# The experts of a two-layer backbone as one list of weight tiles, with fixed places for small operations and a fourth split buffer

## The chip, the cores and the metric

The kernel runs on one NeuronCore of a Trainium2 chip. The metric is the device time of one execution in microseconds. Five engines work beside one another: PE (TensorE) multiplies, VectorE (DVE) and ScalarE (ACT) do elementwise work, GpSimd (POOL) is almost unused here, and SyncE (SP) issues the transfers. Each engine runs its instructions in the order of its own list and waits in that list.

## The reference, cut to what matters

Two layers of a hybrid backbone for 256 latent and 256 context tokens of width 1024. The change is in the last block of the second layer, a top-2-of-8 mixture of SwiGLU experts over the 256 latent tokens:

```python
logits = (xs @ router_w) + router_b
top_val, top_idx = lax.top_k(logits, 2)
gates = sum(one_hot(top_idx, 8) * softmax(top_val)[..., None], axis=-2)
for e in range(8):                       # w_gate, w_up 1024 x 2816, w_down 2816 x 1024, float32
    y = y + gates[..., e:e + 1] * ((silu(xs @ w_gate[e]) * (xs @ w_up[e])) @ w_down[e])
```

The 24 weight matrices are 277 MB of float32, read once each.

## The kernel before, in words

**Precision.** A float32 product is made from float32r products of two parts: `hi` is the value rounded to float32r and `lo` the rest. `hilo` (line 634) makes them from a loaded tile `raw`: ScalarE copies to `hi` (L635), then VectorE subtracts to `lo` (L636). For each weight tile of 128 x 2048 (1 MB) there is one transfer, one `hi` and one `lo`. The buffers are rings: six for `raw`, three for `hi` and three for `lo` in the expert stage (`open_ring(st, 6, 3, 2048)`). A `hi` buffer is free when the products that read it have ended, a `raw` buffer when its `lo` is made.

**Experts.** `route` (line 1421) counts the tokens of each expert and sorts the experts by count. The first four in that order are *big* ones (places for 128 tokens), the other four *small* (64 tokens). A big expert's tokens are the stationary operands `xghi` and `xglo`, so each slice of a tile takes three matmuls: `xghi` by `hi`, `xghi` by `lo`, `xglo` by `hi`. A small expert has both parts of its 64 tokens side by side in one operand `xs`, and takes two matmuls a slice; the halves are added afterwards by a matmul with `sum2`. They run in turn: big 0, small 4, big 1, small 5 and so on.

`gather` (line 1543) makes a one-hot matrix from the places and multiplies it with the tokens, for a big and a small expert at once. `expert_up` (line 1586) goes through six chunks of columns; a chunk of 512 columns has two gate tiles and two up tiles. After a big chunk: `h` = silu(gate) on ScalarE, times up on VectorE (L1632, L1633), four transposes on PE (L1635), and a split into `hT` (L1639, L1640). After a small one: copies `h` and `u` of both sums (L1615, L1616), the sums on PE (L1619), silu and product `g` (L1622, L1623), and a split into `hS` (L1628, L1629). `expert_down` (line 1645) takes eleven tiles. Its tiles are interleaved with the next expert's up tiles, one after every two: `experts` (line 1503) drives both as generators. `scatter` (line 1672) adds the result to the residual with another 16 matmuls.

**What sets the order.** The program only gives a priority, its order of tracing. A planner places each instruction on its engine's list by a cost model, dependencies and free buffers, and can so move a small operation ahead of or behind others. `prefetch` (line 1255) loads the first three tiles into buffers of another pool, ahead of the router; with the six `raw` buffers nine tiles are loaded early.

Of the kernel before, what the change touches and what calls it, by code (L numbers as in the profile page):

```python
# [9 lines left out]
F32 = mybir.dt.float32  # L10
# [10 lines left out]
KD = 8  # L21
# [141 lines left out]
class Kernel:  # L163
# [175 lines left out]
    def ssq_add(self, pool, tag, bank, m, segs, bufs=3, direct=False):  # L339
        nc = self.nc  # L340
        n = segs[-1][1]
        sq = pool.tile([P, T], F32, tag=tag, name="nsq", bufs=bufs)[:, :n]
# [844 lines left out]
    def odd_out(self, od):  # L1187
# [6 lines left out]
        self.sorted = self.mp.tile([P, 6, NE], F32, name="sorted")  # L1194
        self.ints = self.mp.tile([P, 1 + 2 * NE], I32, name="ints")
        self.y2 = [flat[1][:, i * D:i * D + D] for i in range(2)]
        with ExitStack() as st:
# [28 lines left out]
            def back(m, ps):  # L1226
                r = self.resl[:, m]
                nc.vector.scalar_tensor_tensor(r, ps, mix[2][:, m, 0:1], r, op0=ALU.mult, op1=ALU.add)
                xm = yp.tile([P, L], F32, tag="xg", name="xg", bufs=3)
                nc.scalar.activation(xm, r, AF.Copy, scale=gs[:, m, 0:1])  # L1230
                self.ssq_add(yp, "sq", ssq, m, [(0, L, r)])
# [22 lines left out]

    def prefetch(self):
        self.ahead = {}
        for i in range(3):
            src = ("m_gate", "m_up")[i // 2]
            self.ahead[src, i % 2] = self.load(self.I[src][i % 2], self.mp, "big", 3)
# [161 lines left out]
    def route(self, xp, lg, cm, tag):  # L1421
# [35 lines left out]
        pg = tile_(6, NE)  # L1457
# [3 lines left out]
        nc.vector.tensor_scalar(pos, pos, -1.0, None, op0=ALU.add)  # L1461
        nc.vector.tensor_copy(pg[:, 4], cm["order"])
# [14 lines left out]
        nc.vector.tensor_tensor(pg[:, 2:4], rr, den[:, :, None].to_broadcast([P, 2, NE]), op=ALU.mult)  # L1477
# [4 lines left out]
        self.pos, self.gate = self.sorted[:, 0:2], self.sorted[:, 2:4]  # L1482
# [3 lines left out]
        ints = xp.tile([P, 1 + 2 * NE], I32, name="ints")  # L1486
# [7 lines left out]
        nc.vector.tensor_copy(self.ints, ints)  # L1494
# [7 lines left out]

    def experts(self, wk):
        got = {0: self.gather(wk, self.pos, 0, NB)}
        order = [p + NB * s for p in range(NB) for s in range(2)]
        down, todo = iter(()), None
        for n, p in enumerate(order):
            small, i = divmod(p, NB)
            x, hT = got[i][small], []
            for c, _ in enumerate(self.expert_up(wk, p, x, hT)):  # L1510
                if c == 0 and todo:
                    self.scatter(wk, *todo)
                    todo = None
                if c == 2 and small and i + 1 < NB:
                    got[i + 1] = self.gather(wk, self.pos, i + 1, NB + i + 1)
                for done in down:
                    todo = done
                    break
            for done in down:
                todo = done  # L1520
            down = self.expert_down(wk, p, x, hT)
        self.scatter(wk, *todo)
        for todo in down:
            pass
        self.scatter(wk, *todo, "gu")
        self.finish(wk)

    def overflow(self, wk):
        with self.tc.If(self.most > 0):
            for p in range(NE):  # L1530
                over = self.nc.values_load(self.ints[0:1, 1 + NE + p:2 + NE + p], min_val=0, max_val=L)
                with self.tc.If(over > 0):
                    pos = wk.tile([P, 2, NE], F32, tag="pos2", name="pos2", bufs=1)
                    self.nc.vector.tensor_scalar(pos, self.pos, float(-P if p < NB else -64), None, op0=ALU.add)
                    x, hT = self.gather(wk, pos, p, None)[0], []
                    for _ in self.expert_up(wk, p, x, hT, False):
                        pass
                    for todo in self.expert_down(wk, p, x, hT, False):
                        pass
                    self.scatter(wk, *todo)  # L1540
            self.finish(wk)

    def gather(self, wk, pos, p, s):
        nc = self.nc
        mm = nc.tensor.matmul
        cm = self.cm
        hot = wk.tile([P, 2, 2, P], F32R, tag="hot", name="hot", bufs=2)
        both = [(1, p, "slot")] + ([] if s is None else [(0, s, "slot2")])
        for b in range(2):
            for i, e, slot in both:  # L1550
                nc.vector.tensor_scalar(hot[:, b, i], cm[slot], pos[:, b, e:e + 1], None, op0=ALU.is_equal)
        xg = [wk.tile([P, KD, P], F32R, tag="xg" + n, name="xg" + n, bufs=1) for n in ("hi", "lo")]
        xs = None if s is None else wk.tile([P, KD, P], F32R, tag="xs", name="xs", bufs=2)
        cols = slice(0, 2) if xs is not None else slice(1, 2)
        for j, (src, dst) in enumerate(zip((self.thi, self.tlo), xg)):
            for k in range(0, KD, 2):
                ps = self.bank("tr").rearrange("p (k i w) -> p k i w", k=2, i=2)
                for kk in range(2):
                    c = slice((k + kk) * P, (k + kk + 1) * P)
                    for b in range(2):  # L1560
                        mm(ps[:, kk, cols], lhsT=src[:, b, c], rhs=hot[:, b, cols], start=b == 0, stop=b == 1)
                parts = [(dst[:, k:k + 2], ps[:, :, 1])]
                if xs is not None:
                    parts.append((xs[:, k:k + 2, 64 * j:64 * j + 64], ps[:, :, 0, 0:64]))
                for o, i in parts:
                    if j:
                        nc.vector.tensor_copy(o, i)
                    else:
                        nc.scalar.activation(o, i, AF.Copy)
        ps = self.bank("tr").rearrange("p (i b w) -> p i b w", i=2, b=2)  # L1570
        hotT = wk.tile([P, 2, L], F32R, tag="hotT", name="hotT", bufs=2)
        for i, _, _ in both:
            for b in range(2):
                nc.tensor.transpose(ps[:, i, b], hot[:, b, i].bitcast(F32), self.ident)
        nc.scalar.activation(hotT[:, cols], ps[:, cols].rearrange("p i b w -> p i (b w)"), AF.Copy)
        ps = self.bank("tr")
        for i, e, _ in both:
            for b in range(2):
                mm(ps[:, i:i + 1], lhsT=hot[:, b, i].bitcast(F32), rhs=self.gate[:, b, e:e + 1], start=b == 0,
                   stop=b == 1)  # L1580
        gs = wk.tile([P, 2], F32, tag="gslot", name="gslot", bufs=2)
        nc.vector.tensor_copy(gs[:, cols], ps[:, cols])
        big = (xg, hotT[:, 1], gs[:, 1:2])
        return [big] if xs is None else [big, ((xs,), hotT[:, 0], gs[:, 0:1])]

    def expert_up(self, wk, p, now, hT, ahead=True):
        nc = self.nc
        mm = nc.tensor.matmul
        xg = now[0]
        small = len(xg) == 1  # L1590
        for c in range(6):
            width, ks = (512, 4) if c < 5 else (256, 8)
            pgu = []
            for name in ("m_gate", "m_up"):
                ps = self.bank("gu")
                for t in range(8 // ks):
                    j = 2 * c + t
                    raw = self.ahead.pop((name, j), None) if ahead and p == 0 else None
                    whi, wlo = self.weights(None if raw is not None else self.wsrc(name, p, j), ks, raw)
                    for k in range(ks):  # L1600
                        kk = t * ks + k
                        o = ps[:, :width]
                        mm(o, lhsT=xg[0][:, kk], rhs=whi(k), start=kk == 0, stop=False)  # L1603
                        mm(o, lhsT=xg[0][:, kk], rhs=wlo(k), start=False, stop=small and kk == 7)  # L1604
                        if not small:
                            mm(o, lhsT=xg[1][:, kk], rhs=whi(k), start=False, stop=kk == 7)  # L1606
                pgu.append(ps)
                if c < 5:
                    yield
            n = width // P  # L1610
            h = wk.tile([P, 512], F32, tag="h", name="h", bufs=2)
# [117 lines left out]
```

## Time and profile before

| | us |
|---|---|
| median of 3 runs | 1937.38 |
| their range | 1935.64 to 1937.73 |
| the profiled execution | 1935.74 |
| its span, first to last instruction | 1933.9 |

All times in rows are microseconds from the start of the span, and durations in microseconds unless they are marked ns. A row of a timeline has start, duration, engine, line, operation, the tiles it writes and reads, the number of instructions merged into it, and in brackets the idle time ahead of it with what ended it. The end of a matmul is modelled, so the start of the next one tells more than its duration. PEld is the weight load of PE, which runs ahead of the matmuls.

### The profile page before, as it was taken

What the parts mean: (1) busy time and instruction counts of PE and PEld (TensorE: products, weight loads), DVE (VectorE), ACT (ScalarE), POOL (GpSimd) and SP (SyncE); (2) the same over time, 40 slices, a digit from 0 to 9 for tenths busy, and PEclk for the clock granted to TensorE, in tenths of its full rate; (3) what the DMA queues carried; (4) which work ended last, traced back from release to release, by engine and by line L of the source; (5) the groups of instructions that cost most, each with busy time, mean ns of one, the idle gap of its engine ahead of it and who ended that gap; (6) DMA issues with size and microseconds to landing.
All of it is one profiled execution on the core that took longest, in us unless ns stands there. A gap on an engine that the chain in (4) does not pass through costs nothing.

```text
span 1933.9 us, 28843 instructions
## 1 busy us (share of the span) xinstructions
PE 1768.6 (91%) x11628; PEld 1390.4 (72%) x11628; DVE 1445.9 (75%) x1966; ACT 1006.3 (52%) x1131; POOL 90.3 (5%) x92
## 2 busy tenths in 40 slices
PE   6989999698999999989999879989999899998996
PEld 3657776377888888778876768777777677777775
DVE  4577888657995383456685678888888889888987
ACT  3433325635232222366562357776677677767774
POOL 0011102200000000002110000000000000000000
PEclk8999999798999999989999889999999999999997
DMA  7232111325666163123203339999999999989993
GB/s 291 91 111 88 46 42 49 109 88 200 236 238 239 66 223 125 66 80 109 87 23 146 144 133 359 363 344 363 345 341 363 353 346 341 370 335 360 352 380 119
DMA packets 57310, 409.32 MB, mean 212 GB/s; under 512 B 6480, under 2 KB 6864, under 8 KB 8016
## 3 DMA queue, kind: packets, MB, share of 16 engines
q1 hardware_dynamic: 57168, 407.39, 56.5%
q8 instruction: 93, 1.52, 0.3%
q14 instruction: 49, 0.40, 0.1%
HBM read 406.32 MB, written 1.05 MB: 211 GB/s over the span
## 4 chain that ended last, share of the span: by engine, by line
PE 71%; DVE 17%; ACT 7%; issue 4%; POOL 1%; DMA 0%; SPq 0%; DVEq 0%; ACTq 0%; POOLq 0%
DVE lo L636 10%; PE bank_gu L1604 6%; PE bank_b L234 6%; PE bank_b L235 6%; PE bank_b L236 6%; PE bank_gu L1603 5%; ACT hi L635 5%; PE bank_mm L234 4%; PE bank_mm L235 4%; PE bank_mm L236 4%; PE bank_gu L1606 3%; PE bank_dn L1660 3%; PE bank_dn L1659 2%; PE bank_dn L1662 1%; PE bank_tr L1619 1%
## 5 line engine op out<-in xcount | busy, mean ns | idle before, releaser
L636 DVE TENSOR_TENSOR lo<-raw,hi 128x2048 fp32r<-128x2048 f32 (+1 forms) x398 | 765.4, 1946 | 186.3 <-ACT hi L635 184.2
L635 ACT ACTIVATE hi<-raw 128x2048 fp32r<-128x2048 f32 (+1 forms) x398 | 641.3, 1632 | 276.0 <-PE bank_b L235 140.5
L1604 PE MATMUL bank_gu<-lo,xghi 128*128 128x512 f32 (+1 forms) x384 | 148.9, 388 | 27.2 <-DVE lo L636 26.7
L1604 PE MATMUL bank_gu<-lo,xs 128*128 128x512 f32 (+1 forms) x384 | 146.2, 387 | 7.5 <-DVE lo L636 6.4
L1603 PE MATMUL bank_gu<-hi,xghi 128*128 128x512 f32 (+1 forms) x384 | 145.6, 379 | 0.0
L1606 PE MATMUL bank_gu<-hi,xglo 128*128 128x512 f32 (+1 forms) x384 | 144.5, 376 | 0.0
L1603 PE MATMUL bank_gu<-hi,xs 128*128 128x512 f32 (+1 forms) x384 | 144.3, 382 | 0.2
L234 PE MATMUL bank_b<-xhi,hi 128*128 128x512 f32 x352 | 138.0, 394 | 2.9 <-ACT xhi L635 2.9
L234 PE MATMUL bank_mm<-xhi,hi 128*128 128x512 f32 (+1 forms) x320 | 120.9, 380 | 21.5 <-ACT hi L635 15.3
L235 PE MATMUL bank_b<-xlo,hi 128*128 128x512 f32 x352 | 137.9, 392 | 0.0
L236 PE MATMUL bank_b<-xhi,lo 128*128 128x512 f32 x352 | 137.6, 391 | 0.0
L236 PE MATMUL bank_mm<-xhi,lo 128*128 128x512 f32 (+1 forms) x320 | 118.3, 370 | 2.9 <-DVE lo L636 2.1
L235 PE MATMUL bank_mm<-xlo,hi 128*128 128x512 f32 (+1 forms) x320 | 119.7, 374 | 0.0
L1604 PEld LDWEIGHTS bank_gu<-lo,xghi 128*128 128x128 f32 x384 | 72.2, 188 | 54.0 <-DVE lo L636 41.6
L1604 PEld LDWEIGHTS bank_gu<-lo,xs 128*128 128x128 f32 x384 | 72.4, 188 | 32.6 <-DVE lo L636 21.2
L312 DVE SCALAR_TENSOR_TENSOR ada<-ada_raw,sT,ada 128x1024 f32<-128x1024 f32 x70 | 87.2, 1282 | 5.5 <-DMA ada_raw<-in_ada_v 4.8
L234 PEld LDWEIGHTS bank_mm<-xhi,hi 128*128 128x128 f32 x320 | 62.4, 196 | 37.2 <-ACT hi L635 16.5
L1603 PEld LDWEIGHTS bank_gu<-hi,xghi 128*128 128x128 f32 x384 | 72.3, 188 | 13.5
L1603 PEld LDWEIGHTS bank_gu<-hi,xs 128*128 128x128 f32 x384 | 72.4, 188 | 12.4 <-ACT hi L635 1.5
L1606 PEld LDWEIGHTS bank_gu<-hi,xglo 128*128 128x128 f32 x384 | 72.4, 188 | 12.2
L234 PEld LDWEIGHTS bank_b<-xhi,hi 128*128 128x128 f32 x352 | 66.5, 189 | 17.0 <-ACT xhi L635 3.2
L1660 PE MATMUL bank_dn<-lo,hT 128*128 128x512 f32 x176 | 72.8, 414 | 6.2 <-DVE lo L636 6.2
(512 smaller groups left out, 3461.0 us busy)
## 6 DMA issues: line engine op xcount, KB each, us to landing
raw<-in_m_up SPq DMA_DIRECT2D x88, 1024.0 KB, 7.2
raw<-in_m_gate SPq DMA_DIRECT2D x88, 1024.0 KB, 7.1
raw<-in_m_down SPq DMA_DIRECT2D x88, 1024.0 KB, 7.3
ada_raw<-in_ada_v SPq DMA_DIRECT2D x28, 1024.0 KB, 4.9
raw<-in_ada SPq DMA_DIRECT2D x20, 1024.0 KB, 6.0
raw<-in_o_in SPq DMA_DIRECT2D x16, 1024.0 KB, 4.9
raw<-in_w_in SPq DMA_DIRECT2D x12, 1024.0 KB, 4.9
raw<-in_f_gate SPq DMA_DIRECT2D x11, 1024.0 KB, 5.8
```

The costliest lines, as they stand in the source:

```text
L234: mm(out, lhsT=whi, rhs=xhi, start=start, stop=False)
L235: mm(out, lhsT=whi, rhs=xlo, start=False, stop=False)
L236: mm(out, lhsT=wlo, rhs=xhi, start=False, stop=stop)
L312: nc.vector.scalar_tensor_tensor(acc[r], w[:, k], s, acc[r], op0=ALU.mult, op1=ALU.add)
L635: self.nc.scalar.activation(hi, x, AF.Copy)
L636: (self.nc.gpsimd if pool else self.nc.vector).tensor_tensor(lo, x, hi.bitcast(F32), op=ALU.subtract)
L1603: mm(o, lhsT=xg[0][:, kk], rhs=whi(k), start=kk == 0, stop=False)
L1604: mm(o, lhsT=xg[0][:, kk], rhs=wlo(k), start=False, stop=small and kk == 7)
L1606: mm(o, lhsT=xg[1][:, kk], rhs=whi(k), start=False, stop=kk == 7)
L1619: mm(ps[:, 256 * i + 64 * j:256 * i + 64 * j + 64], lhsT=t[:, j * P:(j + 1) * P], rhs=self.cm["sum2"], start=True, stop=True)
L1659: mm(py[a], lhsT=h[0], rhs=whi(i)[:, half[a]], start=f == 0, stop=False)
L1660: mm(py[a], lhsT=h[0], rhs=wlo(i)[:, half[a]], start=False, stop=len(h) == 1 and f == FT - 1)
```

## The change

The tiles of all experts become one list, `tiles()`, in the same order as before (two up tiles, one down tile of the expert before). `pipeline` walks it. At step n it emits what is due ahead of the split, then the split of tile n+3, the transfer of tile n+9, the products of tile n, what is due behind them, and one step of a queue of gather and scatter pieces. `pin` is `keep_in_program_order`: the instruction may not be placed ahead of the one traced before it on its engine. It stands at the splits, the products and the small operations of the stage; the transfers are not pinned. The split rings get a fourth buffer each. The gather of expert 0 is made alone, from the unsorted places (expert 0 is always first), and its one-hot operations are traced ahead of the sort; the first small expert's gather is a second one, of which one step runs per tile. Some work buffers change: `xs` lies in freed space of `flat[0]`, `u` and `hot` have one buffer, `hotT` and `gslot` three, `g` uses `h`, and the squares buffer of the router's norm is 256 wide. The path for more tokens than places (`overflow`) is rewritten likewise; its branch does not run in the trace.

```diff
-    def hilo(self, hi, lo, x, pool=False):
-        self.nc.scalar.activation(hi, x, AF.Copy)
-        (self.nc.gpsimd if pool else self.nc.vector).tensor_tensor(lo, x, hi.bitcast(F32), op=ALU.subtract)
+    def hilo(self, hi, lo, x, pool=False, pin=lambda ins: ins):
+        pin(self.nc.scalar.activation(hi, x, AF.Copy))
+        pin((self.nc.gpsimd if pool else self.nc.vector).tensor_tensor(lo, x, hi.bitcast(F32), op=ALU.subtract))
...
+        nc.vector.tensor_tensor(pg[:, 2:4], rr, den[:, :, None].to_broadcast([P, 2, NE]), op=ALU.mult)
+        self.hots = {}
+        self.hot(0, pg, 0, None)
         nc.vector.tensor_copy(pg[:, 4], cm["order"])
...
+    LEAD = 3
+
+    def prefetch(self):
+        jobs = self.tiles()
+        self.raws = {m: self.fetch(jobs[m], self.mp, "big", 3) for m in range(3)}
+        for m in range(3, 9):
+            self.raws[m] = self.fetch(jobs[m])
+        self.halves = {m: self.split(self.raws.pop(m), lambda ins: ins) for m in range(self.LEAD)}
+
     def experts(self, wk):
...
+        self.got = {p: {} for p in range(NE)}
+        for f in self.gather(wk, 0, self.plain, 0, None):
+            f()
+        self.pipeline(wk, self.tiles(), True)
         self.finish(wk)
+
+    def pipeline(self, wk, jobs, main=False):
...
+        lead, ring = self.LEAD, 9 if main else 6
...
+        if main:
+            self.hot(1, self.sorted, None, NB)
+            queue += self.gather(wk, 1, self.sorted, None, NB)
+        n = 0
+        while n < len(jobs) or queue or any(m >= n for m in list(pre) + list(post)):
+            for f in pre.pop(n, ()):
+                f()
+            if n + lead < len(jobs):
+                halves[n + lead] = self.split(raws.pop(n + lead), pin)
+            if n + ring < len(jobs):
+                raws[n + ring] = self.fetch(jobs[n + ring])
+            if n < len(jobs):
+                name, p, c, t, k = jobs[n]
+                for where, slot, f in self.product(wk, jobs[n], halves.pop(n), n):
+                    {"pre": pre, "post": post, "queue": queue}[where].setdefault(slot, []).append(f) \
+                        if where != "queue" else queue.extend(f)
+                if main and name == "m_gate" and p >= NB and p < NE - 1 and c == 1 and t == 0:
+                    i = p - NB + 1
+                    self.hot(i, self.sorted, i, NB + i)
+                    queue += self.gather(wk, i, self.sorted, i, NB + i)
+            for f in post.pop(n, ()):
+                f()
+            if queue:
+                more = queue.pop(0)()
+                if more:
+                    pre.setdefault(n + 1, []).append(more)
+            n += 1
...
+        def part(j, k):
+            src = (self.thi, self.tlo)[j]
+            ps = self.bank("tr").rearrange("p (k i w) -> p k i w", k=2, i=2)
+            for kk in range(2):
+                c = slice((k + kk) * P, (k + kk + 1) * P)
+                for b in range(2):
+                    pin(mm(ps[:, kk], lhsT=src[:, b, c], rhs=hot[:, b], start=b == 0, stop=b == 1))
...
+            def turn():
+                got["ps"] = ps = self.bank("tr")
+                for i, a in enumerate((h, u)):
+                    for j in range(m):
+                        pin(mm(ps[:, 256 * i + 64 * j:256 * i + 64 * j + 64], lhsT=a[:, j * P:(j + 1) * P],
+                               rhs=self.cm["sum2"], start=True, stop=True))
...
+            return [("pre", n + 1, first), ("post", n + 1, turn), ("pre", n + 2, second), ("pre", n + 3, third)]
...
+        return [("pre", n + 1, first), ("post", n + 1, turn), ("pre", n + 2, second)]
...
+        steps = [lambda: None] + [lambda m=m: back(m) for m in range(0, KD, 2)]
+        return [("pre", n + 1, take), ("queue", 0, steps)]
...
-            self.open_ring(st, 6, 3, 2048)
+            self.open_ring(st, 6, 4, 2048)
```

For a small expert `first` is the two copies `h` and `u`, `second` the silu and product `g`, `third` the split into `hS`. For a big one `first` is `h`, `turn` the four transposes and `second` the split into `hT`. The two `return` lines are those of a small and of a big chunk, the last one is that of the last down tile. A gather has ten steps (eight parts, the transposes of the one-hot, the gates), a scatter four.

## Rows read from the trace of the kernel before

**Rows 1.** The page's first part: busy us of each engine, share of the span, instructions.

```profile
PE 1768.6 (91%) x11628; PEld 1390.4 (72%) x11628; DVE 1445.9 (75%) x1966; ACT 1006.3 (52%) x1131; POOL 90.3 (5%) x92
```

**Rows 2.** Stretches: length, busy PE, PEld, DVE, ACT, POOL; clock, DMA share, GB/s.

```profile
1129.08:1196.59 67.51, 67.51 (x338) 56.05 (x337) 55.18 (x44) 48.00 (x37) 0.00 (x0) 1.00 0.78 287
1196.59:1290.97 94.38, 90.65 (x461) 72.70 (x459) 83.92 (x65) 69.95 (x61) 0.00 (x0) 1.00 0.95 368
...
1389.89:1489.07 99.18, 93.61 (x474) 74.50 (x472) 88.42 (x71) 72.10 (x63) 0.00 (x0) 1.00 0.94 352
1489.07:1588.04 98.97, 89.91 (x416) 70.94 (x414) 84.97 (x56) 68.01 (x48) 0.00 (x0) 1.00 0.94 348
...
1786.24:1883.50 97.26, 90.91 (x437) 70.09 (x436) 86.69 (x64) 71.55 (x55) 0.00 (x0) 1.00 0.95 366
1883.50:1912.20 28.70, 24.99 (x99) 17.94 (x97) 26.29 (x21) 18.30 (x13) 0.00 (x0) 0.94 0.50 186
```

**Rows 3.** Waits, 1150 to 1934 us: total us, times, longest us.

```profile
DVE lo L636 <- ACT hi L635: 72.9, 87, 2.4
PEld bank_gu L1604 <- DVE lo L636: 62.9, 76, 3.1
...
PEld bank_dn L1660 <- DVE lo L636: 20.2, 30, 2.9
```

**Rows 4.** Groups by line and shape, 1080 us on: busy us, mean ns, idle before.

```profile
L635 ACT ACTIVATE hi<-raw 128x2048 fp32r<-128x2048 f32 x265 | 499.3, 1912 | 59.3 <-PE bank_gu L1606 29.5 <-PE bank_gu L1603 11.6 <-PE bank_dn L1659 6.5
...
L1622 ACT ACTIVATE g<-bank_tr 128x256 f32<-128x256 f32 x20 | 7.7, 385 | 37.8 <-PE bank_tr L1619 37.8
```

**Rows 5.** Timeline of VectorE through one chunk of a small expert.

```profile
1238.51 6.69 DVE L636 TENSOR_TENSOR lo<-raw,hi 128x2048 fp32r<-128x2048 f32 x3 [1.35 <-ACT hi L635]
...
1250.12 0.41 DVE L1623 TENSOR_TENSOR g<-g,bank_tr 128x256 f32<-128x256 f32 x1
1250.95 2.29 DVE L636 TENSOR_TENSOR lo<-raw,hi 128x2048 fp32r<-128x2048 f32 x1 [0.41 <-ACT hi L635]
...
1254.93 6.70 DVE L636 TENSOR_TENSOR lo<-raw,hi 128x2048 fp32r<-128x2048 f32 x3 [1.35 <-ACT hi L635]
```

**Rows 6.** Timeline of PE: transposes, sums, and products in a row.

```profile
1144.79 0.66 PE L1635 MATMUL bank_tr<-const_base,h 128*128 128x128 f32 x4
1145.20 0.48 PE L1604 MATMUL bank_gu<-lo,xghi 128*128 128x512 f32 x1
...
1247.69 1.00 PE L1619 MATMUL bank_tr<-const_moe,u 128*128 128x64 f32 x8
1248.50 0.47 PE L1603 MATMUL bank_gu<-hi,xs 128*128 128x512 f32 x1
1248.81 0.39 PE L1604 MATMUL bank_gu<-lo,xs 128*128 128x512 f32 x1
...
1250.90 0.40 PE L1603 MATMUL bank_gu<-hi,xs 128*128 128x512 f32 x1
```

**Rows 7.** Timeline of VectorE through one chunk of a big expert.

```profile
1342.65 0.69 DVE L1633 TENSOR_TENSOR h<-h,bank_gu 128x512 f32<-128x512 f32 x1 [0.72 <-PE bank_gu L1606]
...
1347.38 6.70 DVE L636 TENSOR_TENSOR lo<-raw,hi 128x2048 fp32r<-128x2048 f32 x3 [1.11 <-ACT hi L635]
1355.01 4.49 DVE L636 TENSOR_TENSOR lo<-raw,hi 128x2048 fp32r<-128x2048 f32 x2 [0.93 <-ACT hi L635]
1360.21 0.69 DVE L1633 TENSOR_TENSOR h<-h,bank_gu 128x512 f32<-128x512 f32 x1 [0.71 <-PE bank_gu L1606]
```

**Rows 8.** Timeline of VectorE ahead of the first expert: places, then one-hot.

```profile
1119.37 0.17 DVE L1461 TENSOR_SCALAR rt<-rt 128x16 f32<-128x16 f32 x1
...
1124.61 1.66 DVE L1551 TENSOR_SCALAR hot<-const_moe,sorted 128x128 fp32r<-128x128 f32 x8 [0.47 <-DVE ints L1494]
```

**Rows 9.** Waits of SP's own queue, 1150 to 1900 us.

```profile
SPq L214 <- DVE lo L636: 487.4, 200, 6.2
```

**Rows 10.** A stretch of 10 us inside the stage.

```profile
1210.00:1220.00 10.00, 10.00 (x57) 8.54 (x56) 7.66 (x8) 7.97 (x13) 0.00 (x0) 1.00 1.01 420
```

More of the change, by code (lines that the diff above doesn't have):

```diff
@@ L1501, in wsrc, with parts @@
         return src.rearrange("(e j) p c -> j e p c", j=11)[j, bass.ds(self.ids[p], 1)].rearrange("e p c -> (e p) c")
-    def experts(self, wk):
[L1504 to L1525, printed above, removed]
-        self.finish(wk)
+    def parts(self, p):
+        up = [("m_gate" if t < k else "m_up", p, c, t % k, k) for c in range(6) for k in (2 if c < 5 else 1,)
+              for t in range(2 * k)]
+        return up, [("m_down", p, c, 0, 1) for c in range(FT // 2)]
@@ new lines, in tiles, with fetch @@
+    def tiles(self):
+        order = [p + NB * s for p in range(NB) for s in range(2)]
+        jobs, down = [], []
+        for n, p in enumerate(order):
+            up, mine = self.parts(p)
+            first = len(jobs)
+            for g in range(FT // 2):
+                jobs += up[2 * g:2 * g + 2] + down[g:g + 1]
+            down = mine
+        return jobs + down
+    def fetch(self, job, pool=None, tag="raw", bufs=None):
+        name, p, c, t, k = job
+        return self.load(self.wsrc(name, p, c if name == "m_down" else 2 * c + t), pool, tag, bufs)
@@ new lines, in experts @@
+    def experts(self, wk):
+        self.got = {p: {} for p in range(NE)}
+        for f in self.gather(wk, 0, self.plain, 0, None):
+            f()
+        self.pipeline(wk, self.tiles(), True)
+        self.finish(wk)
+    def pipeline(self, wk, jobs, main=False):
+        pin = self.tc.keep_in_program_order
+        raws, halves = (self.raws, self.halves) if main else ({}, {})
+        lead, ring = self.LEAD, 9 if main else 6
+        if not main:
+            for m in range(min(6, len(jobs))):
+                raws[m] = self.fetch(jobs[m])
+            for m in range(min(lead, len(jobs))):
+                halves[m] = self.split(raws.pop(m), pin)
+        pre, post, queue = {}, {}, []
+        if main:
[25 more added lines that the diff above has]
+            n += 1
@@ new lines, in product_down, with take, back, out @@
+    def product_down(self, wk, job, w, n):
+        nc, pin = self.nc, self.tc.keep_in_program_order
+        mm = nc.tensor.matmul
+        _, p, c, _, _ = job
+        now = self.got[p]
+        half = [slice(a * 512, a * 512 + 512) for a in range(2)]
+        if c == 0:
+            now["py"] = [self.bank("dn") for _ in range(2)]
+        py, last = now["py"], c == FT // 2 - 1
+        order = [(i, a) for i in range(2) for a in range(2)]
+        if last:
+            order.sort(key=lambda o: o[1])
+        for i, a in order:
+            f = 2 * c + i
+            h = now["h"][f]
+            whi, wlo = [x[:, i * D + a * 512:i * D + a * 512 + 512] for x in w]
+            pin(mm(py[a], lhsT=h[0], rhs=whi, start=f == 0, stop=False))
+            pin(mm(py[a], lhsT=h[0], rhs=wlo, start=False, stop=len(h) == 1 and f == FT - 1))
+            if len(h) == 2:
+                pin(mm(py[a], lhsT=h[1], rhs=whi, start=False, stop=f == FT - 1))
+        if not last:
+            return []
+        y, gs, hotT = self.y2, now["gs"], now["hotT"]
+        def take():
+            for a in range(2):
+                pin(nc.scalar.activation(y[0][:, half[a]], py[a], AF.Copy, scale=gs))
+                pin(nc.vector.scalar_tensor_tensor(y[1][:, half[a]], py[a], gs, y[0][:, half[a]].bitcast(F32),
+                                                   op0=ALU.mult, op1=ALU.subtract))
+        def back(m):
+            ps = self.bank("tr").rearrange("p (m t) -> p m t", m=2)
+            for i in range(2):
+                s = slice((m + i) * P, (m + i + 1) * P)
+                pin(mm(ps[:, i], lhsT=y[0][:, s], rhs=hotT, start=True, stop=False))
+                pin(mm(ps[:, i], lhsT=y[1][:, s], rhs=hotT, start=False, stop=True))
+            def out():
+                for i in range(2):
+                    r = self.resl[:, m + i]
+                    pin(nc.vector.scalar_tensor_tensor(r, ps[:, i], self.gain[:, m + i, 0:1], r, op0=ALU.mult,
+                                                       op1=ALU.add))
+            return out
+        steps = [lambda: None] + [lambda m=m: back(m) for m in range(0, KD, 2)]
+        return [("pre", n + 1, take), ("queue", 0, steps)]
@@ L1540, in overflow @@
-                    self.scatter(wk, *todo)
-            self.finish(wk)
[L1543 to L1584, printed above, removed]
@@ L1672, in scatter @@
[L1672 to L1683 removed]
+                    pos = wk.tile([P, 4, NE], F32, tag="pos2", name="pos2", bufs=1)
@@ new lines, in overflow @@
+                    self.nc.vector.tensor_scalar(pos[:, 0:2], self.sorted[:, 0:2], float(-P if p < NB else -64), None,
+                                                 op0=ALU.add)
+                    self.nc.vector.tensor_copy(pos[:, 2:4], self.sorted[:, 2:4])
+                    self.hot(2, pos, p, None)
+                    self.got[p] = {}
+                    for f in self.gather(wk, 2, pos, p, None):
+                        f()
+                    up, down = self.parts(p)
+                    self.pipeline(wk, up + down)
```

239 lines of the change are left out of this document (123 added, 116 removed).

## The prediction

> **What bounds the kernel now.** I read the page's busy shares first, then the expert stage cut by phase, then the waits, then one chunk of each kind. The change touches the eight experts, 264 weight tiles of 1 MB from about 1129 us on; everything ahead of the router stays. Over the whole span PE is busy 91% and VectorE 75% [rows 1], which says little, since the stage has its own limits. Cut where the stationary operand changes from one expert to the next [rows 2], there is a first phase of 67.5 us (22 tiles), then seven phases of 33 tiles, small experts (one operand holding both halves of 64 tokens) and big ones (128 tokens) in turn: 94.4, 98.9, 99.2, 99.0, 99.2, 99.0 and 97.3 us, together 687.0. (Phases of 98.9, 99.2 and 99.0 that aren't shown repeat their neighbours.) Then 28.7 us of the last down tiles.
>
> The first phase has PE busy for all of its 67.51 us. In the seven others nothing is full: VectorE 83.9 to 88.4 us, ScalarE 68 to 72, and PE, whose busy time includes modelled ends, about 90 to 94. What ends PE's idle time is nearly always the split: the weight load waits for `lo` 62.9 us in the up products and 20.2 in the down products, while `lo` itself waits 72.9 us for `hi` [rows 3]. That is a closed ring: `hi` waits for PE to free one of three split buffers, `lo` for `hi`, PE for `lo`. `hi` takes 1.91 us [rows 4] and `lo` 2.29, 2.2 apart in a row [rows 5], so 4.1 us pass between the end of a product and the split that reuses its buffer. With three buffers PE has two products to fill that with, 2 x 2.8 us for big ones but 1.9 for the small, and any small operation that gets in front of a split eats the rest.
>
> **The change part by part.** *Fourth split buffer, lead of three.* The split for tile n+3 starts when product n-1 ends, so three products lie between. I walk through a chunk (six tiles: four up, two down).
>
> Big chunk. PE: 4 x 12 + 2 x 8 = 64 matmuls of 512 columns, each 0.232 us (nine steps from 1248.81 to 1250.90 [rows 6]), 14.85, and four transposes 0.41 [rows 6], 15.26. VectorE today: a period of 17.56 us with 1.11, 0.93 and 0.71 idle [rows 7], so 14.8 of work. The transposes now stand at a fixed place behind the next product. Their `h` comes behind the split that was under way: 1.91 + 2.2 after the product before, less 2.8 for one product, is 1.3 us, and 0.6 for the multiply makes 1.95; the small down product that covers it lasts 8 x 0.232 = 1.86. PE so waits 0.1 to 0.2. A chunk is 15.5 instead of 17.56, bound by PE.
>
> Small chunk. PE: 56 x 0.232 + two groups of eight sums at 0.81 [rows 6] = 14.6. VectorE: a period of 16.42 with 1.35 and 0.41 idle [rows 5], 14.66 of work. Here the fixed places bring a chain that I charge: the copy of `u` on VectorE, then the sums of `u` on PE (0.81; those of `h` are ahead of it), then `g` on ScalarE (0.39 [rows 4]), and only behind it, in ScalarE's kept order, the next `hi` (1.91): 3.1 us, in which VectorE has one `lo` and one multiply, 2.2 + 0.3 [rows 5]. It idles 0.6 to 0.7 a chunk. If all sixteen sums stood behind the copy, it would be 1.6, which is today's idle time. I take 0.7, since `h` leaves ScalarE before the `u` copy can start: 15.4 instead of 16.42, bound by VectorE.
>
> Phases, 5.5 chunks each. Big: 5.5 x 15.5 = 85.3, 16 scatter matmuls of half width at about 0.116 us, 1.9, and 1 us for the change of phase, 88.2; VectorE's 85.0 fits under it. Small: VectorE's busy 88.4 (with gather and scatter) + 5.5 x 0.7 = 92.3; the first 83.9 + 3.9 = 87.8, the last 86.7 + 3.9 = 90.6 [rows 2]. Sum 87.8 + 3 x 88.2 + 2 x 92.3 + 90.6 = 627.6, against 687.0: 59.4 us less, inside the 83 us of PE's waits for `lo`.
>
> *Gather one step per tile, scatter one step per tile.* Per pair of phases 10 gather steps, 8 scatter steps and 12 turns, each behind a product on PE and each evacuated ahead of the next split, from two banks. What is queued behind a waiting step is all of PE. No row shows such a kept order. From below the cost is nothing, where the evacuation fits beside the next product (1.86 or 2.8 us); from above one whole `lo`, 2.2 us a step. I take 1 us a phase, near the lower end, because VectorE comes to the step within one product as shown for the transposes: +7.
>
> *Start.* The one-hot of expert 0 is made from the unsorted places: they exist after 1119.4, while today `hot` starts at 1124.61, behind the sort [rows 8]. Four operations make the gather start some 4 us earlier. Against it, the small expert's gather is no longer in the same matmuls: 32 x 0.116 + transposes and gates, about 5 us more on PE in the phase that PE fills [rows 2]. Net 0, between -4 and +5. The first three splits are already made ahead of the router today, in gaps of VectorE, and stay there at no cost.
>
> *Transfers.* Same queue, same count, nine tiles ahead at the start, then six buffers as today; each issue moves behind the split that frees its buffer, which is where SP waits now (487 us for `lo` [rows 9]), so SP gets no new wait. With all engines busy the stage reached 420 GB/s over 10 us [rows 10]: 2.5 us a tile, 15.0 a chunk, below 15.4. The gates' move, the narrower squares buffer and the fewer work buffers cost nothing that lies on this path. *Tail:* down tiles at VectorE's 2.2 us, as now: 0.
>
> Sum: -59.4 + 7 + 0 = -52. The profiled execution took 1935.74 us (span 1933.9 and 1.8 around it), 1.6 below the median of the runs: 1935.7 - 52 = 1883.7, as a median about 1885.
>
> **The Trainium skill on the transfers.** The seven phases move 348 to 368 GB/s at a DMA share of 0.94 to 0.95 [rows 2], which looks full. The Trainium skill, DMA: Bandwidth & Descriptors, section "Where 436 GB/s comes from", says that for transfers from HBM the memory's share of a core, about 358 GB/s, binds, and not the ports. By that rule 264 tiles want some 773 us, an estimate from the page, and the change would bring nothing. The trace disagrees where it can: 420 GB/s over 10 us inside the stage.
>
> **The rivals.** (a) The transfers bind. If what the phases show, 350 GB/s, is what the memory gives beside busy engines, 33 tiles take 99 us whatever the order: 1937. For it: every phase after the first small one has the same 99 us. Against: SP waits for free buffers, no `hi` waits for data, 368 GB/s in the first small phase. 0.06. (b) Slower: the steps at fixed places stop PE. Thirty steps a pair stand in PE's queue, and each needs VectorE to have got through a split first. PE's own work in a pair is 85.3 + 1.9 + 5.5 x 14.6 + 6 of gather and scatter, some 174; today's pair takes 198. From 24 / 30 = 0.8 us a step the change loses. At 1.0 us a pair takes 204, +6 x 3.5 = 21: 1958; at 2.2 us 240, +147: 2084. For it: VectorE is the fullest engine of the small phases, so it will be late. Against: by my walk turns wait 0.2 to 0.4. 0.11. (c) Small chunks gain nothing, because the sums' chain idles VectorE for 1.6 us as now: 0.9 x 5.5 = 5 us a small phase more than I take, 4 x 5 = 20: 1905. For it: today's 0.41 and 1.35 of idle time come from that same chain. 0.21. (d) All waits go, and each phase falls to the larger of VectorE's busy time and PE's work: 83.9 + 85.8 + 88.4 + 85.8 + 88.4 + 85.8 + 86.7 = 604.8, -82: 1855 (85.8 is 5.5 x 15.26 + 1.9). 0.10.
>
> **How the numbers follow.** Forecast 0.52, at 1866 to 1900. The range of eight in ten goes from (d) to beyond (c), since steps of 0.6 us would, by (b), leave 174 + 18 = 192 us a pair and 1916: 1854 to 1922. What a measurement of this kernel can tell from no change is about 0.2%, 4 us. Faster: the forecast, (c), (d): 0.83 and a little of the rest, 0.84. Same: (a), 0.05. Slower: (b), 0.11.
>
> **What would show it.** Big phases of 88 us and small ones of 92; PE's waits for `lo` under 20 us; instead of them waits of PE's sums and transposes for `u` and `h`. VectorE's waits for `hi` remaining in small phases beside `g`. SP waiting less, DMA near 390 GB/s. Wrong it is if the big phases stay near 99, if scatter and gather matmuls wait a microsecond each, or if `hi` begins to wait for data.

## The result, and the profile after

| | before | after |
|---|---|---|
| median, us | 1937.56 (1935.64 to 1939.35, 4 runs) | 1892.1 (1889.41 to 1894.38, 4 runs) |
| ratio | | 0.9765, 95% interval 0.9748 to 0.9782 |
| profiled execution, us | 1935.74 | 1894.38 |
| its span, us | 1933.9 | 1892.6 |
| span from the router's first sum to the end, us | 817.4 | 775.1 |

The change makes the kernel 2.3% faster. The last row is used below to compare profiles: the router's first sum, which comes behind the same work everywhere, lies between 1113.6 and 1120.1 us in the fourteen profiles, so spans differ by up to 6.5 us for reasons ahead of the experts. I call it the stage. Each stage is that of one profile, and the part behind the last down matmul alone varies from 20.8 to 23.7 us over the fourteen, so a difference of 2 or 3 us between two stages says little by itself.

The first part of the page, in answer to [rows 1]: busy us of each engine, share, instructions.

```profile
PE 1753.4 (93%) x11660; PEld 1404.6 (74%) x11660; DVE 1445.0 (76%) x1970; ACT 1003.4 (53%) x1132; POOL 88.9 (5%) x92
```

Nearly the same work is done in less time. The stage by phase, to be held against [rows 2]: length, then busy PE, PEld, DVE, ACT, POOL, the clock, the DMA share and GB/s. The first row is the first big phase, then small and big ones in turn.

```profile
1133.41:1201.59 68.18, 68.18 (x348) 56.97 (x348) 56.39 (x46) 49.02 (x39) 0.00 (x0) 1.00 0.84 307
...
1291.87:1382.15 90.28, 87.54 (x417) 70.60 (x416) 85.15 (x57) 69.38 (x48) 0.00 (x0) 1.00 0.99 381
1382.15:1477.79 95.64, 91.12 (x474) 77.15 (x474) 88.35 (x74) 70.58 (x61) 0.00 (x0) 0.98 0.95 365
...
1568.19:1661.64 93.45, 89.27 (x474) 75.81 (x474) 87.60 (x70) 70.45 (x61) 0.00 (x0) 1.00 0.97 373
```

Phases of 99 us became 90.3 (big) and 93.5 to 95.6 (small), the first small one went from 94.4 to 90.3; the middle six together went from 589.65 to 550.33. The last small phase and the down tiles behind it give 7.8 more, and the first small phase begins 5.0 us later than before: -39.3 - 7.8 + 5.0 + 0.9 of the end is the 41.3 by which the spans differ, but for rounding.

The waits of the stage, in answer to [rows 3]: engine, line, what it waited for, us in total, times, longest.

```profile
ACT h L1693 <- PE bank_tr L1688: 69.1, 24, 4.9
ACT hi L635 <- PE bank_gu L1666: 50.9, 75, 1.5
DVE lo L636 <- ACT hi L635: 49.9, 87, 1.8
ACT hT L1718 <- PE bank_tr L1714: 25.7, 24, 2.2
...
PE bank_tr L1688 <- DVE u L1682: 12.5, 18, 1.4
PE bank_tr L1714 <- DVE h L1709: 8.6, 16, 1.6
```

The weight load's 83 us of waiting for `lo` are gone (0.7 us in two waits is left). In their place PE waits for `u` and `h` in front of the sums and transposes, as forecast. `hi` still waits 50.9 us for PE to free a buffer. One small chunk on VectorE, against [rows 5], and one big, against [rows 7]: start, duration, operation, idle time ahead and what ended it.

```profile
1452.43 0.68 DVE L1682 COPY u<-bank_gu 128x512 f32<-128x512 f32 x1
1453.03 2.28 DVE L636 TENSOR_TENSOR lo<-raw,hi 128x2048 fp32r<-128x2048 f32 x1
1455.23 0.41 DVE L1694 TENSOR_TENSOR h<-h,bank_tr 128x256 f32<-128x256 f32 x1
1456.60 2.29 DVE L636 TENSOR_TENSOR lo<-raw,hi 128x2048 fp32r<-128x2048 f32 x1 [0.95 <-ACT hi L635]
1458.80 0.42 DVE L1699 TENSOR_TENSOR hS<-h,hS 128x256 fp32r<-128x256 f32 x1
1459.14 8.89 DVE L636 TENSOR_TENSOR lo<-raw,hi 128x2048 fp32r<-128x2048 f32 x4
1467.95 0.69 DVE L1682 COPY u<-bank_gu 128x512 f32<-128x512 f32 x1
...
1511.55 0.68 DVE L1709 TENSOR_TENSOR h<-h,bank_gu 128x512 f32<-128x512 f32 x1
...
1515.41 4.62 DVE L636 TENSOR_TENSOR lo<-raw,hi 128x2048 fp32r<-128x2048 f32 x2 [0.38 <-ACT hi L635]
1520.54 4.49 DVE L636 TENSOR_TENSOR lo<-raw,hi 128x2048 fp32r<-128x2048 f32 x2 [0.51 <-ACT hi L635]
1525.20 2.29 DVE L636 TENSOR_TENSOR lo<-raw,hi 128x2048 fp32r<-128x2048 f32 x1 [0.17 <-ACT hi L635]
1527.40 0.68 DVE L1709 TENSOR_TENSOR h<-h,bank_gu 128x512 f32<-128x512 f32 x1
```

A small chunk lasts 15.52 us (`u` to `u`) and idles once, 0.95 behind `g`; a big one lasts 15.85 (`h` to `h`). Forecast were 15.4 with 0.6 to 0.7, and 15.5.

### The profile page after: what moved, and what is told of

The parts are those of the page before. It is cut to its first block, busy times and chain, and to the rows that moved or that the text cites. A ratio compares the mean times of both kernels' runs of the same rounds, so it can differ in the third digit from the quotient of the medians.

```text
span 1892.6 us, 28958 instructions
## 1 busy us (share of the span) xinstructions
PE 1753.4 (93%) x11660; PEld 1404.6 (74%) x11660; DVE 1445.0 (76%) x1970; ACT 1003.4 (53%) x1132; POOL 88.9 (5%) x92
## 4 chain that ended last, share of the span: by engine, by line
PE 68%; DVE 18%; issue 6%; ACT 6%; POOL 1%; DMA 0%; SPq 0%; DVEq 0%; ACTq 0%; POOLq 0%
DVE lo L636 8%; PE bank_b L234 6%; PE bank_b L235 6%; PE bank_b L236 6%; PE bank_gu L1663 5%; PE bank_gu L1664 5%; PE bank_mm L234 4%; PE bank_mm L235 4%; PE bank_mm L236 4%; ACT hi L635 4%; PE bank_gu L1666 3%; PE bank_dn L1740 2%; PE bank_dn L1739 2%; PE bank_tr L1688 2%; PE bank_tr L1606 1%
## 5 line engine op out<-in xcount | busy, mean ns | idle before, releaser
L1663 PE MATMUL bank_gu<-hi,xhi 128*128 128x512 f32 (+1 forms) x384 | 144.6, 383 | 0.0
L1664 PE MATMUL bank_gu<-lo,xghi 128*128 128x512 f32 (+1 forms) x384 | 144.0, 375 | 0.0
L1664 PE MATMUL bank_gu<-lo,xhi 128*128 128x512 f32 (+1 forms) x384 | 142.0, 377 | 0.0
L234 PE MATMUL bank_mm<-xhi,hi 128*128 128x512 f32 (+1 forms) x320 | 120.5, 379 | 22.5 <-ACT hi L635 15.4
L1663 PEld LDWEIGHTS bank_gu<-hi,xhi 128*128 128x128 f32 x384 | 73.4, 191 | 11.8
L1664 PEld LDWEIGHTS bank_gu<-lo,xhi 128*128 128x128 f32 x384 | 73.4, 191 | 11.6
L274 PE MATMUL bank_mm<-hi,xhi 128*128 128x256 f32 x256 | 73.6, 287 | 4.1 <-DVE yo L1159 2.2
```

The source lines that it names most:

```text
L234: mm(out, lhsT=whi, rhs=xhi, start=start, stop=False)
L274: mm(ps, lhsT=xhi[:, k, t], rhs=whi(k), start=k == 0, stop=False)
L1663: pin(mm(o, lhsT=x[0][:, kk], rhs=whi[:, s], start=kk == 0, stop=False))
L1664: pin(mm(o, lhsT=x[0][:, kk], rhs=wlo[:, s], start=False, stop=small and kk == 7))
```

## The experiments

All are edits of the changed kernel unless said; ratios are to the kernel before, run on the same chip. By my theory the fourth buffer carried the gain; the rival was the kept order. Four kernels separate them, with the start.

**Buffers without the fourth, order kept.**

```diff
-            self.open_ring(st, 6, 4, 2048)
+            self.open_ring(st, 6, 3, 2048)
-    LEAD = 3
+    LEAD = 2
```

> Three split buffers and a lead of two, order kept. Theory (the fourth buffer carries the gain): the closed ring hi waits for PE, lo for hi, PE for lo is back, and the kept order puts g and the copies in front of splits: PE waits for lo 60 us or more in the stage, the phases are 97 to 102 us, the time 1930 to 1960. Rival (the kept places carry it): PE waits for lo under 15 us, time 1890 to 1905.

Measured: 1903.18 us, ratio 0.9804 (0.9786 to 0.9822), stage 787.8. A big phase is 90.29, as with four buffers, a small one 95.9 to 96.7 (the first one 93.5):

```profile
1294.67:1384.96 90.29, 87.55 (x416) 70.58 (x416) 85.00 (x57) 69.37 (x48) 0.00 (x0) 1.00 0.98 379
```

What three buffers cost lies in small phases and at the end: the weight load of the down products waits 34.9 us for `lo`, and the last down tiles take 33.9 us instead of 31.4. My theory failed: three buffers in kept order bring 30 of the 42 us that the stage gains. The rival's time came true, its bound on the waits for `lo` (15 us) did not.

**Order left to the planner, with four buffers and with three.** In both, `pin` becomes the identity; the second has the edit above as well.

```diff
-        pin = self.tc.keep_in_program_order
+        pin = lambda ins: ins
```

> Four split buffers and the list, but no instruction is kept in program order. Theory: the ring is open, so PE waits for lo stay under 20 us; the planner also moves the register load behind the gather, which gives 4 to 5 us at the start: 1880 to 1900. Rival (the kept order carries the gain): phases of 95 us and more, 1920 to 1940.

> Three split buffers, lead of two, nothing kept in program order: the list, the separate gather and the small work buffers alone. Theory (buffer): 1930 to 1945, PE waits for lo 60 us or more, as before the change. Rival (the list and the new places of gather and scatter bring the gain themselves): under 1910.

Measured: four buffers 1932.66, ratio 0.9966 (0.9954 to 0.9978), stage 812.2; three 1930.61, 0.9953 (0.9935 to 0.9971), stage 813.0. For three buffers the time fits, for four the rival holds, with big phases of 97.2 us:

```profile
1291.30:1388.54 97.24, 89.78 (x417) 70.78 (x416) 84.61 (x57) 66.97 (x48) 0.00 (x0) 1.00 0.95 352
```

The stage as a square: free order 813.0 with three buffers and 812.2 with four, kept order 787.8 and 775.1. In the free order the fourth buffer is worth nothing that can be told (0.8 us, and the ratios lie the other way), in the kept order 12.7 us by the stage and some 7.6 by the ratios. The list, the separate gather and all else of the change bring 4.4 us by the stage, 817.4 to 813.0, and some 9 by the ratio.

Why the fourth buffer lay idle is to be read from ScalarE in a big chunk of the free order with four buffers:

```profile
1512.97 0.60 ACT L1708 ACTIVATE h<-bank_gu 128x512 f32<-128x512 f32 x1 [2.36 <-PE bank_gu L1666]
1513.47 5.51 ACT L635 ACTIVATE hi<-raw 128x2048 fp32r<-128x2048 f32 x3
1522.93 0.60 ACT L1718 ACTIVATE hT<-bank_tr 128x512 fp32r<-128x512 f32 x1 [3.95 <-PE bank_tr L1714]
1523.42 5.51 ACT L635 ACTIVATE hi<-raw 128x2048 fp32r<-128x2048 f32 x3
1530.57 0.60 ACT L1708 ACTIVATE h<-bank_gu 128x512 f32<-128x512 f32 x1 [1.64 <-PE bank_gu L1666]
```

and from PE in the same chunk, where the last row waits for the `lo` of such a late `hi`:

```profile
1517.20 0.39 PE L1666 MATMUL bank_gu<-hi,xglo 128*128 128x512 f32 x1
...
1522.29 0.60 PE L1714 MATMUL bank_tr<-const_base,h 128*128 128x128 f32 x4
...
1526.24 0.40 PE L1663 MATMUL bank_gu<-hi,xghi 128*128 128x512 f32 x1
1527.70 0.50 PE L1664 MATMUL bank_gu<-lo,xghi 128*128 128x512 f32 x1 [1.07 <-DVE lo L636]
```

The planner put `hT` ahead of three splits on ScalarE's list. ScalarE reaches it at 1518.98 and stands 3.95 us, until the transposes at 1522.29, which PE has behind a down product. The `hi` that follows at 1523.42 is for the product at 1526.24; four products earlier, its buffer's last reader began its last matmul at 1517.20. So that buffer was free while ScalarE stood at `hT`. With two such stops (3.95 at `hT`, 1.64 at `h`) a chunk lasts 17.60 us (`h` at 1512.97 to `h` at 1530.57). The kernel before shows the same two, 1.64 and 3.37, and 17.56 from one `hT` to the next (ScalarE, then one row of PE):

```profile
1525.52 0.60 ACT L1639 ACTIVATE hT<-bank_tr 128x512 fp32r<-128x512 f32 x1 [3.17 <-PE bank_tr L1635]
1526.01 5.51 ACT L635 ACTIVATE hi<-raw 128x2048 fp32r<-128x2048 f32 x3
1533.15 0.60 ACT L1632 ACTIVATE h<-bank_gu 128x512 f32<-128x512 f32 x1 [1.64 <-PE bank_gu L1606]
...
1543.08 0.60 ACT L1639 ACTIVATE hT<-bank_tr 128x512 fp32r<-128x512 f32 x1 [3.37 <-PE bank_tr L1635]
...
1522.79 0.39 PE L1606 MATMUL bank_gu<-hi,xglo 128*128 128x512 f32 x1
```

There too a buffer was free, with three of them: the `hi` at 1526.01 is for the product that begins at 1528.81, and the product three earlier began its last matmul at 1522.79, more than 2 us before ScalarE could go on at `hT`.

**Whose order: ScalarE's alone, and all but ScalarE's.** In the second, `==` is `!=`.

```diff
+    def pin(self, ins):
+        if ins.ins.engine == mybir.EngineType.Activation:
+            self.tc.keep_in_program_order(ins)
+        return ins
```

> Four buffers and lead three; only ScalarE's instructions are kept in program order, all other engines are left to the planner. Theory (the planner puts hT, g and h ahead of splits whose buffer is already free, and ScalarE stands at them): ScalarE's waits for the transposes fall from 59 us to under 30, big phases to 89 to 92 us, time 1890 to 1905. Rival (the kept places on PE or VectorE carry as much): 1915 to 1932.

> Four buffers and lead three; every engine but ScalarE is kept in program order. Theory: ScalarE stands at hT and g as in the free order, waits for the transposes 45 us or more, big phases 95 to 97 us, time 1918 to 1935. Rival (the order of the other engines is enough): under 1905.

Measured: ScalarE alone 1898.94, ratio 0.9802 (0.9786 to 0.9819), stage 781.0, big phases 91.6; all but ScalarE 1910.85, 0.9856 (0.9833 to 0.9879), stage 791.2, big phases 91.2, small ones 92 to 101. From the free order's 812.2, ScalarE's order brings 31 us, that of the others 21, both 37 (counted from the first product, to leave the start out, 31, 26 and 41): each mends much of what the other does, since the planner moves the free lists along with the kept ones. These pairs show that the order is the cause of the gain; that it acts through ScalarE's list is read from the two traces above. Several of my numbers missed. All but ScalarE kept came out between the two forecasts, with big phases of 91.2 instead of 95 to 97 and 19.3 us of waits at `hT` instead of 45 or more, and with ScalarE kept its waits at `hT` rose from 59.0 to 73.4 us instead of falling. A big chunk there has one long stop at `hT` (4.1), but five splits run in a row behind it and `h` costs no stop, so VectorE's waits for `hi` fall from 72.0 us to 40.7. How long ScalarE waits is thus no measure by itself; what seems to count is whether a split with a free buffer stands behind it and VectorE has run out.

**The start.** The register load of `most`, on all engines, is traced at the head of `overflow` instead.

```diff
-        self.most = nc.values_load(ints[0:1, 0:1], min_val=0, max_val=L)
...
     def overflow(self, wk):
+        self.most = self.nc.values_load(self.ints[0:1, 0:1], min_val=0, max_val=L)
```

> The register load of most (on all engines) is traced behind the experts instead of ahead of the first gather. Theory: PE's first gather starts at 1121 to 1122 instead of 1126.4, the first product at 1128 to 1129 instead of 1133.4, phases unchanged: 4 to 5 us less than the changed kernel, 1887 to 1888. Rival (the first product then waits for something else, or the load costs as much at the end): 1891 to 1893.

Measured: 1891.3, ratio 0.9751 (0.9734 to 0.9768), which the time alone doesn't separate from the changed kernel. The trace does. PE in the changed kernel, from the router's sums on:

```profile
1117.46 0.60 PE L1447 MATMUL bank_mm<-rt,const_moe 128*128 128x8 f32 x2 [7.03 <-DVE rt L1437]
...
1126.44 1.20 PE L1606 MATMUL bank_tr<-hot,xhi 128*128 128x256 f32 x4 [6.67 <-DVE ints L1488]
...
1133.41 0.48 PE L1663 MATMUL bank_gu<-hi,xghi 128*128 128x512 f32 x1
```

and with the late load:

```profile
1116.97 0.59 PE L1447 MATMUL bank_mm<-rt,const_moe 128*128 128x8 f32 x2 [7.03 <-DVE rt L1437]
...
1120.79 1.37 PE L1605 MATMUL bank_tr<-hot,xhi 128*128 128x256 f32 x4 [1.52 <-DVE hot L1583]
...
1125.59 1.23 PE L1605 MATMUL bank_tr<-hot,xlo 128*128 128x256 f32 x4 [1.72 <-DVE xglo L1615]
...
1130.80 0.48 PE L1662 MATMUL bank_gu<-hi,xghi 128*128 128x512 f32 x1
```

The gather starts 5.2 us earlier against the router's sums, but the first product only 2.1 (13.83 instead of 15.95 us behind them): the gather now waits for VectorE's copies, which come behind the whole sort (the first runs at 1125.12), as the first half of the rival said. The stage is 771.0, 4.1 us less, but 1.7 of that lie behind the last down matmul, where profiles differ by more than that. My 4 to 5 was too much. The 13.8 came again in the two late-load kernels further down.

**Moving one small operation at a time.** First the transposes of a big chunk, one product later.

```diff
-        return [("pre", n + 1, first), ("post", n + 1, turn), ("pre", n + 2, second)]
+        return [("pre", n + 1, first), ("post", n + 2, turn), ("pre", n + 3, second)]
```

> All kept; the four transposes of a big chunk stand one product later on PE, and the split into hT one step later. Theory (PE's waits for h, 3.6 us a big phase, are what a big phase has above PE's own work): big phases 86.5 to 87.5 us instead of 90.3, time 1878 to 1884. Rival (VectorE with 85.2 us of work, or the transfers, take over): big phases 89 to 90.5, 1888 to 1893.

Measured: 1876.06, ratio 0.9689 (0.9672 to 0.9706), stage 760.5. Big phases are 86.1 us and PE is busy for all of it, as this row shows (columns as for the phases above):

```profile
1288.15:1374.28 86.13, 86.13 (x414) 70.99 (x414) 83.65 (x55) 68.53 (x48) 0.00 (x0) 1.00 1.00 398
```

The theory holds, with a little more than it forecast, and the transfers keep up with 398 GB/s at a DMA share of 1.00.

Then `g` of a small chunk behind the split of its step; the split into `hS` stayed where it was, and no queue step ran in that step.

```diff
-            return [("pre", n + 1, first), ("post", n + 1, turn), ("pre", n + 2, second), ("pre", n + 3, third)]
+            return [("pre", n + 1, first), ("post", n + 1, turn), ("mid", n + 2, second), ("pre", n + 3, third)]
```

> All kept; in small experts silu and product g stand behind the split of their step instead of ahead of it, and no gather or scatter step runs in that step (both banks are then in use). Theory (the chain sums, g, next hi idles VectorE 0.95 us a chunk): that wait is gone, the small phases go from 93 to 96 us to 89 to 92, time 1874 to 1884. Rival (PE or the transfers bind these phases): 1887 to 1893.

Measured: 1923.04, ratio 0.9923 (0.9909 to 0.9936), stage 805.8. Worse by 31 us, with neither theory right. ScalarE in one of its small chunks:

```profile
1455.59 0.42 ACT L1701 ACTIVATE hS<-h 128x256 fp32r<-128x256 f32 x1 [4.66 <-DVE h L1697]
1455.91 3.71 ACT L635 ACTIVATE hi<-raw 128x2048 fp32r<-128x2048 f32 x2
```

The multiply of `g` moved behind a `lo` on VectorE, but `hS`, which reads it, kept its place ahead of the next split on ScalarE. It stands there 70.1 us in 22 waits, and small phases grew to 102 us. So I moved both, on top of the later transposes (in the step `n + 2` no queue step runs, since both banks are in use):

```diff
-            return [("pre", n + 1, first), ("post", n + 1, turn), ("pre", n + 2, second), ("pre", n + 3, third)]
+            return [("pre", n + 1, first), ("post", n + 1, turn), ("hold", n + 2, None),
+                    ("pre", n + 3, second), ("pre", n + 4, third)]
```

> The transposes one product later, as in the run before, and in small experts silu and product g one step later and the split into hS one step after that, so that neither stands where its input is still being made; one queue step of gather or scatter is left out per small chunk (the bank is in use). Theory (the chain sums, g, next hi costs VectorE 0.95 us a chunk, and the last attempt failed only because hS then stood on ScalarE ahead of a product that VectorE had behind a lo): a small chunk 14.6 to 14.9 us instead of 15.5, small phases 90 to 91 instead of 94 to 95, time 1856 to 1864. Rival (the transfers, at a DMA share of 1.00 and 398 GB/s in the big phases, bind next): 1868 to 1876.

Measured: 1870.66, ratio 0.9649 (0.9627 to 0.967), stage 752.8. The time lies in the rival's range, but the chunk in the theory's: a chunk without gather is 14.81 us (`u` at 1444.06 and 1458.87). Small phases fell from 94.7 and 94.1 to 92.3, not to 90 to 91; in the chunks with gather steps VectorE still waits for `hi`, once 1.74 us. The transfers did not bind: no `hi` waited for data.

The next two add the late load, and then move the sums of a small chunk too (`turn` at `n + 2`, the hold at `n + 3`, `second` at `n + 4`, `third` at `n + 5`).

> As e9_g_later, with the register load of most behind the experts. Theory: 2 to 3 us less than e9_g_later, first product 1.8 us or more earlier against the router. Rival (no effect on the end): the same time within 1 us.

> As e10_g_later_load, with the sums of a small chunk one product later too, and g and hS again one step later. Theory (PE's waits for u, 11.8 us in all, count where PE binds a small chunk): up to 8 us less than e10_g_later_load. Rival (VectorE binds the small chunk, 14.66 us of work against PE's 14.6): the same within 3 us.

Measured: 1870.91, ratio 0.965 (0.9634 to 0.9667), stage 751.5: no difference in the time, though the first product is 2.1 us earlier; one small phase was 1.6 us longer. With the sums later as well 1866.65, ratio 0.9622 (0.9605 to 0.9638), stage 747.4, 4.1 less. The 11.8 us in its forecast are those of the kernel with the later transposes alone; in the one it builds on PE waited 4.0 us for `u`, and now 0.8. Small phases fell to 90 to 91 us, two of the big ones grew from 86.2 to 87.7, which was not looked into. By its median this is the fastest kernel of the study, 3.8% below the kernel before, and below the changed one without an overlap of intervals. Its small chunk is 14.47 us without a gap on VectorE:

```profile
1443.47 0.68 DVE L1681 COPY u<-bank_gu 128x512 f32<-128x512 f32 x1
1444.07 6.68 DVE L636 TENSOR_TENSOR lo<-raw,hi 128x2048 fp32r<-128x2048 f32 x3
1450.67 0.41 DVE L1693 TENSOR_TENSOR h<-h,bank_tr 128x256 f32<-128x256 f32 x1
1451.00 2.28 DVE L636 TENSOR_TENSOR lo<-raw,hi 128x2048 fp32r<-128x2048 f32 x1
1453.20 0.42 DVE L1698 TENSOR_TENSOR hS<-h,hS 128x256 fp32r<-128x256 f32 x1
1453.54 4.49 DVE L636 TENSOR_TENSOR lo<-raw,hi 128x2048 fp32r<-128x2048 f32 x2
1457.94 0.68 DVE L1681 COPY u<-bank_gu 128x512 f32<-128x512 f32 x1
```

**The price of a gather or scatter step.** The changed kernel again, with the queue served at every second tile.

```diff
-            if queue:
+            if queue and (n % 2 == 0 or n >= len(jobs)):
```

> The changed kernel with one queue step of gather or scatter at every second tile instead of at every tile. Theory (a gather step costs more than its own work, because ScalarE stands at its evacuation ahead of a split: VectorE waits 0.3 to 1.2 us a pair of steps, 3.5 us in a small phase that holds a gather): small phases 92 to 94 us where they were 95.6 and 93.5, big ones unchanged at 90.3, 1884 to 1889. Rival (the steps cost only the work that they bring, wherever they stand): the phases and 1892 as before, within 2 us.

Measured: 1885.9, ratio 0.9717 (0.9697 to 0.9736), stage 765.8. Small phases 93.7 and 91.2 instead of 95.6 and 93.5; the others gained too, 0.6 us a big one, 1.2 the first small one and 1.6 the last, which holds scatter steps alone. The same steps thus cost more than their own work where they follow each other tile by tile. VectorE of the changed kernel in the phase with a gather shows where:

```profile
1407.98 2.29 DVE L636 TENSOR_TENSOR lo<-raw,hi 128x2048 fp32r<-128x2048 f32 x1 [1.19 <-ACT hi L635]
```

Ahead of this row ScalarE stood 1.16 us at a copy of the gather (`xghi`), with the split behind it. Five waits in that phase outside the chain of `g`, four for `hi` and one for a gather matmul, add to 3.5 us.

## Why the prediction was right, and where it wasn't

The number was right: 1885 against 1892.1, inside the range and inside the narrower range of the forecast. The cause that it named first was not.

**"That is a closed ring: `hi` waits for PE to free one of three split buffers"** is the step that failed. A fourth buffer alone left 97 us phases, and the kept order with three buffers reached 90.3. In the two traces shown the wait that set 17.6 us ran through `hT` and `h` on ScalarE's list, while a split buffer was free. I had the half sentence, "any small operation that gets in front of a split eats the rest", but read only the waits along the split; those of ScalarE in the trace of before pointed at the holder:

```profile
ACT hT L1639 <- PE bank_tr L1635: 54.8, 22, 3.4
ACT g L1622 <- PE bank_tr L1619: 41.4, 22, 2.8
...
ACT h L1632 <- PE bank_gu L1606: 22.1, 19, 1.6
```

The waits of `hi` for PE in up products do not tell the same: 41.1 us in the trace of before (29.5 and 11.6), but 48.7 with three buffers in kept order and 50.9 with four, in kernels that are faster. The number survived because the chunks were walked with each operation at its new fixed place, so the walk priced the order while the text credited the buffer.

**Big chunk**, 15.5: 15.85. Bound by PE, as said (later transposes give 86.1 with PE full, at 15.36 a chunk where the sum had 15.26). The wait ahead of the transposes was put at 0.1 to 0.2. Moving them gave 4.15 us a phase: by the starts on PE the wait is 0.43 in four of its chunks, and 1.75 in the first (1308.53 to 1310.51), which was not looked into. Mis-sized were the hand-overs: in the chunk shown, 5.10 us pass on PE from the change of product at 1507.19 to the transposes at 1512.29, where the walk had 4.71. The missing parts are 0.20 us until `hi` begins (1507.39), 0.04 from there to `lo` and 0.14 between `h` and the transposes.

**Small chunk**, 15.4: 15.52. The chain of sums, `g` and next `hi` was right in kind, 0.95 instead of 0.6 to 0.7; with it moved away the chunk fell to 14.81. Rival (c), 1.6 a chunk (by its own terms 1.4), is excluded by the row with 0.95.

**"Inside the 83 us of PE's waits for `lo`"** was no bound on the gain: those 83 us are waits of the weight load, which runs beside the matmuls. PE's own waits for `lo` were 33.0 and 5.1 us in the trace of before.

**Gather and scatter steps**, +7: near 9 us could be had by spacing them alone, so the steps cost at least that beyond their own work. Inside my bounds, above my choice. The slower rival (b) needed 0.8 us a step; VectorE's extra waits add to 3.5 us in a phase that holds fourteen steps.

**Start**, 0: +5.0, at my upper end. Against the router's sums the first product went from 12.60 to 15.95 us, and the first phase grew by 0.7; 1.0 arose ahead of the router. Of the 3.35, 2.1 is the register load that I overlooked: it stood on PE's list ahead of the kept gather and waited for the sort, so the early one-hot bought nothing. The rest and the 0.7 go with the separate gather, which I had counted, though no run isolates it: 38 of its matmuls stand ahead of the first product, where 16 of the joint one stood and the other 28 ran among the first products.

**Transfers**, no cost: right. The changed kernel's big phases move 381 to 383 GB/s, later ones 398 for 86 us, and no `hi` of the changed kernel waits for data. Rival (a) is excluded for this kernel, over whole phases and not only over the 10 us of [rows 10]. The Trainium skill (DMA: Bandwidth & Descriptors, section "Where 436 GB/s comes from") gets its bound of about 358 GB/s by halving a memory stack's rate between two cores. The 381 to 398 GB/s of these phases exclude it for this kernel, which runs on one core. **Tail**: 0.9 us longer behind the last down matmul, within what it varies by from profile to profile. SP's waits for `lo` in the stage fell from 507.7 to 423.6 us, as expected.

Summed: the phases were to give 52 and gave 47, the start took 5. What stays open is why keeping every list but ScalarE's mends big phases so well and small ones so badly, and with it which engine's order carries how much.

## What to carry to other kernels

When several engines feed each other through rings, look for the small operation at which an engine stands while a buffer behind it is already free; until that was moved, another buffer bought nothing here. Place each small operation where its input has been made, and when one is moved, move every later link of its chain on the other engines with it. A register load on all engines is an instruction on every list: here it held up PE ahead of a gather that could have begun 5.2 us earlier.

## What the runs showed of the hardware

One core took in 398 GB/s over 86.1 us at a DMA share of 1.00, with PE busy throughout and VectorE for 83.7 us (the row shown with the later transposes); in the fastest kernel it was 404 over 87.7 us. In that kernel, though not in this phase, two `hi` waited for data, 1.1 us together. Whether that is the end, no run here shows: PE and VectorE are both nearly full beside it.
